# Branch B's first weights, its copies out of PSUM and the chunks' sum moved in the order of a hybrid decoder step

## The chip, the cores and the metric

The kernel runs on one core of one Trainium2 chip. The metric is the time of one execution on the device, in microseconds. Three runs of the kernel before took 989.81, 990.08 and 991.59 us; their median is 990.08 us.

## The reference

One layer of a decoder trunk is computed for 16 learned meta tokens with a prompt of 1024 positions, and for 8 sequences of 8 sample tokens; the model width is 1024.

```python
h = rmsnorm(x, norm_g)
z = jnp.einsum('btd,de->bte', h, w_in)
a_val, a_gate, a_silu, p_in, p_silu, g_a, g_b = jnp.split(z, idx, axis=-1)
u = a_val * jax.nn.sigmoid(a_gate)
c, new_conv = causal_depthwise_conv(u, buf_conv, conv_w, conv_b)       # width 31
c = jax.nn.silu(layernorm(c, ln_g, ln_b)) * jax.nn.silu(a_silu)
br_a = jnp.einsum('btc,cd->btd', c, w_conv_out)
pooled, new_pool = multiscale_pool(p_in, buf_pool, start_pos)          # windows 2, 4, 8, 16
q = jnp.einsum('btgc,gce->btge', pg, w_pool_mix).reshape(B_, T_, D_POOL)
q = q * pool_scale * jax.nn.silu(p_silu)
br_b = jnp.einsum('btc,cd->btd', q, w_pool_out)
merged = jax.nn.sigmoid(g_a) * br_a + jax.nn.sigmoid(g_b) * br_b
return x + jnp.einsum('btd,de->bte', merged, w_out), new_conv, new_pool
```

A final RMSNorm follows. The conv and pool states of the prompt and of the samples are outputs too. All inputs are fp32.

## The kernel before, in words

Channels lie on the 128 partitions, so a matrix of 1024 channels is eight chunks. The tokens are kept in two halves (`h` = 0, 1). Every fp32 product is made from three products of parts: each operand is split into a high part, rounded to the type that TensorE takes, and a low part, the rest; high times high, high times low and low times high are added in PSUM (`gemm`, L152). ScalarE's cast makes the high part. The low part comes in one of several ways: `split` (L119) has VectorE subtract at once; `split_late` (L124) has VectorE subtract some steps later; `split_dma` (L130) has ScalarE write the negated high part and a DMA of GpSimd's queue add the source onto it.

PSUM is four tiles of two banks (`bank2`). They are handed out in the order of the program: a new one takes the tile whose last reader came earliest in that order, and its first matmul waits for this reader.

The program is written out in one order by hand, and each engine executes its own instructions in that order. Three helpers make it. `step(us)` stands after each half product of TensorE: it counts a step, adds `us` to a planned TensorE clock and runs what is due. `defer(n, f)` makes `f` due n steps later; what is due in one step runs in the order in which it was deferred. `fill(until)` takes VectorE's background work (a queue `todo` of groups with planned costs: the taps of the depthwise conv, then the layer norm of branch A) until the planned VectorE clock is 1.5 us ahead of the planned TensorE clock; without an argument it takes everything that is queued.

The stages around the change:

- The pairs (L919 to L960). Most of the input projection is made in 22 pairs of column blocks with seven products each (`seven`); the last pair is `s3` (tiles `px_s`, `pv_s`, `py_s`). Beside them VectorE works at the conv. `load_q` reads branch B's `q` back from DRAM, `split_q` splits it. `po[d]` are the eight blocks of branch B's projection, `co[d]` those of branch A's (`Block.load` is two SP loads of 256 KB, `Block.split` makes the operands, tiles `raw_po` and `w_po`).
- Branch B's projection (L1052 to L1072). For each of eight blocks `d` and both halves: two half products of 24 matmuls into one PSUM tile (`ppo`), a `step` after each; then ScalarE copies the tile to SBUF (`zpo`), and SP stores it a step later (`d_tb`), to be read again at the merge. The `fill` calls in this loop place the rest of the conv, the sum over the chunks, the mean (`pt_mean`: an all-ones product), the centring and the squares, the variance (`pt_var`), and the first part of `finish_a`. The sum of the chunks that were stored lies in DRAM (`csum`); `load_sum` reads it, and queues `summing`, which adds the chunks that were kept, and after it the group that begins the mean.
- `finish_a` is `root` (the reciprocal root, and `scale` of chunk 0) and `branch_a(0)` to `branch_a(8)`. `branch_a(i)` scales chunk i+1 (VectorE multiplies, ScalarE takes the Silu), makes the low parts that are left over from the chunk before, loads the gate `lsa` two chunks ahead, multiplies chunk i by its gate and splits it into `cx[i]`.
- After the loop the tail takes what is left:

```python
while todo or due:
    fill()
    step(0.0)
```

- The merge (L1122 on): the first four products of branch A, blocks 0 and 1 with both halves, are made together, k by k, in all four PSUM tiles (`pco`); the other twelve follow one by one. VectorE multiplies each by its gate (L1147) and adds branch B's. Then come the output projection (`pwo`), the residual and the norm.

Of the kernel before, what the change touches and what calls it, by code (L numbers as in the profile page):

```python
# [32 lines left out]
H2 = HP + HS  # L33
# [36 lines left out]
def hybrid_trunk_kernel(  # L70
# [22 lines left out]
    act, dve, pe, pool, sp = nc.scalar, nc.vector, nc.tensor, nc.gpsimd, nc.sync  # L93
# [8 lines left out]
    def slot(name, shape=(T2,), dt=F32):  # L102
        return sl.tile([P, *shape], dt, tag="slot", name=name, bufs=NSLOT)


    def bank2(name):
        return ps2.tile([P, 2, 512], F32, tag="bank2", name=name, bufs=4)
# [34 lines left out]
    def half(name, n=HT, dt=F32):  # L142
        return wp.tile([P, n], dt, tag="z", name=name, bufs=NZ, padded_shape=[P, HT])
# [4 lines left out]
    def v3(ap, n):  # L148
        return ap.rearrange("p (a b) -> p a b", b=n)


    def gemm(out, w, xs, units, ks, first, last):  # L152
        for k in ks:
            for i, (a, b) in enumerate(((0, 0), (0, 1), (1, 0))):
                for u, (lo, hi) in enumerate(units):
                    pe.matmul(  # L156
                        out[:, u, : hi - lo],
                        w(k, a),
                        xs(k, b)[:, lo:hi],
                        start=first and k == ks[0] and i == 0,  # L160
                        stop=last and k == ks[-1] and i == 2,
                        skip_group_check=True,
                    )
# [5 lines left out]
    def defer(steps, run):  # L169
        due.append((clock["step"] + steps, run))  # L170

    def step(us):
        clock["step"] += 1
        clock["pe"] += us
        for x in [x for x in due if x[0] <= clock["step"]]:
            due.remove(x)
            x[1]()
# [147 lines left out]
    for i in range(NF, NX):  # L325
        ps = bank2(f"pp{i}0")
# [79 lines left out]
    def push(group, soon=False):  # L406
        todo.insert(1 if soon and todo else len(todo), deque(group))

    def fill(until=None):
        while todo and (until is None or clock["dve"] < until + LAG):  # L410
            if not todo[0]:
                todo.popleft()
                continue
            cost, run = todo[0].popleft()
            clock["dve"] += cost
            run()
# [53 lines left out]
    def seven(w, units, put):  # L470
# [46 lines left out]
    d_pool, d_q, d_sga, d_sgb, d_sa, d_c, d_tb = (  # L517
        dram.tile([NK, P, 2, H2], F32, name=f"d_{x}") for x in ("pool", "q", "sga", "sgb", "sa", "c", "tb")
    )
# [278 lines left out]
    def of_half(t):  # L798
        return v3(t, H2 // 2)

    def fetch_half(src, h, name):
        t = half(f"{name}{h}", H2)
        sp.dma_start(out=t, in_=src[:, h])
        return t

    def gemm_half(name, w, xs, h, nk):
        ps = bank2(f"{name}{h}")
        gemm(ps, w, lambda k, s: xs[k][h][:, s], UNITS3, tuple(range(nk)), True, True)
        return ps[:, :, : H2 // 2]

    def operand(name, src, how):
        o = slot(name, (2, H2), F32R)
        how(o[:, 0], o[:, 1], src)
        return o
# [45 lines left out]
    po = [Block(w_po[d], f"po{d}") for d in range(NK)]  # L860
# [48 lines left out]
    def load_q(j):  # L909
        qraw[j] = [fetch_half(d_q[j], h, f"lq{j}") for h in range(2)]  # L910

    def split_q(j):
        q.append([operand(f"q{j}{h}", z, split if j > 5 else split_late) for h, z in enumerate(qraw.pop(j))])
# [5 lines left out]
    for n in range(len(pairs)):  # L919
        nxt = pairs[n + 1][1] if n + 1 < len(pairs) else iter(())  # L920
        if n + 1 == len(pairs):
            for j, t in enumerate((1, 1, 2, 2, 3, 4, 5, 5)):
                if j > 1:
                    defer(t - 2, lambda j=j: load_q(j)) if t > 2 else load_q(j)
                defer(t, lambda j=j: split_q(j))
            po[0].load()
            defer(2, lambda: po[0].split(split))
            defer(3, po[1].load)
        next(after, None)
        next(cur)  # L930
        if mix:
            tail = mix.part(0, 0)
        next(cur)
        if mix:
            mix.gate(*tail)
            mix.gate(*mix.part(0, 1))
            mix.split(1)
        if 0 <= n - first_q < 4:
            coming = Mix(n - first_q)
            coming.load(0)  # L940
            coming.load_w()
        next(nxt, None)
        next(cur)
        if mix:
            tails = [mix.part(1, 0), mix.part(1, 1)]
            for tail in tails:
                mix.gate(*tail)
        if n + 2 == len(pairs):
            load_q(0)
            load_q(1)  # L950
        next(cur)
        if coming:
            coming.split(0)
            coming.split_w()
            coming.load(1)
        next(nxt, None)
        next(nxt, None)
        mix, coming = coming, None
        after, cur = cur, nxt
# [6 lines left out]
    def load_sa(i):  # L966
        if i < NK:
            lsa[i] = [fetch_half(d_sa[i], h, f"lsa{i}") for h in range(2)]


    def load_conv(lo, hi):
        for i in range(lo, hi):
            if getattr(chunks[i], "stored", False):
                conv[i] = slot(f"lc{i}", (2, H2))
                sp.dma_start(out=conv[i], in_=d_c[i])

    def load_sum():
        norm["sum"] = slot("lcsum", (2, H2))
        sp.dma_start(out=norm["sum"], in_=csum[0])
        todo.insert(max(len(todo) - 1, 0), deque(summing))  # L980
        push([(1.3, lambda: begin_totals("mean", squares_, norm.pop("parts"), [NK - 1]))])

    def sum_rest(i):
        if not chunks[i].stored:
            conv[i] = chunks[i].c
            dve.tensor_tensor(norm["sum"], norm["sum"], conv[i], ALU.add)
# [5 lines left out]
    def begin_totals(name, work, parts_, more):  # L992
        for i in more:
            if i not in conv:
                conv[i] = chunks[i].c
            parts_ = parts_ + total_parts(conv[i], H2, f"{name}{i}")

        def run():
            norm[name] = total_products(parts_, H2, name)
            push(work)  # L1000

        defer(1, run)
# [16 lines left out]
    def scale(i):  # L1019
        if i < NK:  # L1020
            dve.tensor_tensor(conv[i], conv[i], norm["rstd"], ALU.mult)
            act.activation(conv[i], conv[i], AF.Silu, bias=col(OFF_LB, i), scale=col(OFF_LG, i))
# [3 lines left out]
    def branch_a(i):  # L1026
        scale(i + 1)
        while low:
            low.popleft()()
        if i == NK:  # L1030
            return
        load_sa(i + 2)
        cx.append([])
        for h in range(2):
            src = conv[i][:, h]
            dve.tensor_tensor(src, src, lsa[i][h], ALU.mult)
            if i in (1, 3, 5):
                cx[i].append(operand(f"cx{i}{h}", src, split_dma))
            else:
                o = slot(f"cx{i}{h}", (2, H2), F32R)  # L1040
                act.copy(o[:, 0], src)  # L1041
                low.append(
                    lambda o=o, src=src: dve.tensor_tensor(o[:, 1], src, o[:, 0].bitcast(F32), ALU.subtract)
                )
                cx[i].append(o)
# [3 lines left out]
    squares_.append((1.3, lambda: begin_totals("var", finish_a, total_parts(norm[0], H2, "var"), [])))  # L1049
    summing = [(1.3, lambda i=i: sum_rest(i)) for i in range(NK - 1)] + [(1.3, sum_parts)]  # L1050

    for d in range(NK):  # L1052
        (po + co)[d + 2].load()
        (po + co)[d + 1].split(split_dma)
        for h in range(2):
            ps = bank2(f"ppo{d}{h}")
            for ks in (range(NQ), range(NQ, NK)):
                gemm(ps, po[d], lambda k, s: q[k][h][:, s], UNITS3, tuple(ks), ks[0] == 0, ks[0] > 0)
                step(T_PRODUCT)
                if ks[0] == 0 and d > 0:  # L1060
                    fill(clock["pe"])
            z = half(f"zpo{d}{h}", H2)
            act.copy(of_half(z), ps[:, :, : H2 // 2])  # L1063
            defer(1, lambda d=d, h=h, z=z: sp.dma_start(out=d_tb[d][:, h], in_=z))
            if d == 0:
                load_conv(h * 4, h * 4 + 4)
            if d == 1 and h == 0:
                load_sum()
            if d == 7 and h == 0:
                co[1].split(split_dma)  # L1070
                co[2].load()
            fill(clock["pe"])  # L1072
# [49 lines left out]
    for d in range(NK):  # L1122
# [16 lines left out]
        for h in range(2):  # L1139
            if d < 2:  # L1140
                ps = early[d, h][:, :, : H2 // 2]
            else:
                ps = gemm_half(f"pco{d}", co[d], cx, h, NK)
# [170 lines left out]
```

## Time and profile before

| what | value |
|---|---|
| median of three runs | 990.08 us |
| the profiled execution, its own time | 992.53 us |
| its span | 990.7 us |
| TensorE matmuls, busy | 947.3 us, 96% |
| VectorE busy | 771.8 us, 78% |
| ScalarE busy | 492.1 us, 50% |
| GpSimd busy | 185.7 us, 19% |
| mean granted TensorE clock | 0.976 of full speed |

The busy time of TensorE counts matmuls that overlap each other's start and drain, so it says when TensorE had work, not how fast it was. The granted clock is 1.00 at 2.4 GHz and 0.50 at 1.2 GHz. In the rows below a time is in us from the start of the span. In a timeline a row begins with the start and the duration of a run of like instructions; the bracket at its end is the time in which the engine stood idle before it, and what released it.

### The profile page before, as it was taken

What the parts mean: (1) busy time and instruction counts of PE and PEld (TensorE: products, weight loads), DVE (VectorE), ACT (ScalarE), POOL (GpSimd) and SP (SyncE); (2) the same over time, 40 slices, a digit from 0 to 9 for tenths busy, and PEclk for the clock granted to TensorE, in tenths of its full rate; (3) what the DMA queues carried; (4) which work ended last, traced back from release to release, by engine and by line L of the source; (5) the groups of instructions that cost most, each with busy time, mean ns of one, the idle gap of its engine ahead of it and who ended that gap; (6) DMA issues with size and microseconds to landing.
All of it is one profiled execution on the core that took longest, in us unless ns stands there. A gap on an engine that the chain in (4) does not pass through costs nothing.

```text
span 990.7 us, 18094 instructions
## 1 busy us (share of the span) xinstructions
PE 947.3 (96%) x7040; PEld 924.0 (93%) x7040; DVE 771.8 (78%) x1009; ACT 492.1 (50%) x834; POOL 185.7 (19%) x218
## 2 busy tenths in 40 slices
PE   9999997999999999999999999979999399999996
PEld 8999997999999999999999999969998399998885
DVE  6568959996988998999999999667985858664343
ACT  7655155556446555656556565544247842233111
POOL 0001322323232213223233322302202110000000
PEclk9999998999999999999999999979999599999998
DMA  8323797797968887888979899688547688652223
GB/s 315 131 81 100 235 267 136 169 223 185 230 134 220 208 208 185 227 232 212 235 173 239 179 243 209 183 294 241 142 114 199 192 220 280 189 187 93 85 75 106
DMA packets 104646, 187.61 MB, mean 189 GB/s; under 512 B 21872, under 2 KB 25328, under 8 KB 104560
## 3 DMA queue, kind: packets, MB, share of 16 engines
q1 hardware_dynamic: 70720, 121.98, 37.8%
q0 software_dynamic: 24624, 46.57, 27.4%
q10 hardware_dynamic: 9216, 17.90, 4.8%
q8 instruction: 55, 0.90, 0.4%
q14 instruction: 31, 0.25, 0.1%
HBM read 93.92 MB, written 48.71 MB: 144 GB/s over the span
## 4 chain that ended last, share of the span: by engine, by line
PE 68%; DVE 12%; DMA 9%; ACT 5%; issue 5%; SPq 1%; ACTq 0%; DVEq 0%; POOL 0%; POOLq 0%
PE pco L156 10%; PE pp L156 7%; PE px_b L156 5%; PE px_a L156 5%; PE pwo L1187 4%; PE px_s L156 4%; PE px_v L156 4%; PE px_g L156 4%; DVE c L690 4%; PE ppo L156 3%; PE px_q L156 2%; PE pv_b L156 2%; PE pv_a L156 2%; PE pv_v L156 2%; PE pmix L156 2%
## 5 line engine op out<-in xcount | busy, mean ns | idle before, releaser
L690 DVE SCALAR_TENSOR_TENSOR c<-ce,pv,c 128x1024 f32<-128x1024 f32 x240 | 308.2, 1284 | 11.4 <-ACT c L667 6.2
L156 PE MATMUL pco<-cx,w_co 128*128 128x272 f32 x768 | 102.4, 297 | 16.7 <-ACT cx L1041 12.0
L156 PEld LDWEIGHTS pco<-cx,w_co 128*128 128x128 f32 x768 | 101.3, 197 | 17.7 <-ACT cx L1041 12.2
L156 PE MATMUL ppo<-q,w_po 128*128 128x272 f32 x768 | 96.8, 288 | 0.6 <-DMA w_po<-raw_po 0.6
L156 PEld LDWEIGHTS ppo<-q,w_po 128*128 128x128 f32 x768 | 96.3, 188 | 0.8 <-DMA w_po<-raw_po 0.8
L1187 PE MATMUL pwo<-wo,mx 128*128 128x512 f32 x336 | 79.2, 393 | 0.0
L1187 PEld LDWEIGHTS pwo<-wo,mx 128*128 128x128 f32 x336 | 63.1, 188 | 14.7
L156 PE MATMUL pp<-xg,wh_p 128*128 128x276 f32 x384 | 65.4, 291 | 0.5 <-DVE xg L232 0.3
L156 PEld LDWEIGHTS pp<-xg,wh_p 128*128 128x128 f32 x384 | 54.8, 188 | 1.5 <-DVE xg L232 0.8
L120 ACT CAST mx<-ga 128x544 fp32r<-128x544 f32 x16 | 10.4, 647 | 63.9 <-DVE ga L1148 63.9
L1206 DVE TENSOR_TENSOR xr<-pwo,xr 128x1024 f32<-128x1024 f32 (+1 forms) x9 | 9.9, 1106 | 39.1 <-PE pwo L1187 19.9
L1169 ACT ACTIVATE sq<-xr 128x1024 f32<-128x1024 f32 (+1 forms) x9 | 8.7, 964 | 63.2 <-DVE xr L1206 63.2
L156 PE MATMUL pp<-xg,wl_p 128*128 128x276 f32 x192 | 40.0, 290 | 0.0
L156 PEld LDWEIGHTS pp<-xg,wl_p 128*128 128x128 f32 x192 | 30.2, 188 | 0.0
L1063 ACT COPY zpo<-ppo 128x544 f32<-128x544 f32 x16 | 9.8, 612 | 39.2 <-PE ppo L156 39.1
L133 POOL DMA_DIRECT2D w_po<-raw_po x14 | 12.1, 868 | 88.1 <-ACT w_po L132 85.9
L1147 DVE TENSOR_TENSOR ga<-pco,ga 128x544 f32<-128x544 f32 x16 | 11.5, 722 | 19.2 <-PE pco L156 19.2
L156 PE MATMUL px_g<-tT,woq_g 128*128 128x276 f32 x144 | 21.8, 314 | 4.8 <-ACT py_g L489 4.8
L156 PE MATMUL pmix<-px,m 128*128 128x272 f32 x192 | 26.0, 288 | 0.0
L156 PEld LDWEIGHTS px_g<-tT,woq_g 128*128 128x128 f32 x144 | 21.1, 212 | 5.0 <-ACT py_g L489 5.0
L156 PE MATMUL px_q<-tT,woq_q 128*128 128x272 f32 x192 | 25.5, 288 | 0.3 <-ACT py_q L489 0.3
L156 PE MATMUL px_b<-tT,woq_b 128*128 128x272 f32 x192 | 25.4, 288 | 0.0
(421 smaller groups left out, 2266.9 us busy)
## 6 DMA issues: line engine op xcount, KB each, us to landing
lraw<-d_raw SPq DMA_DIRECT2D x16, 276.0 KB, 3.4
d_pool<-pool SPq DMA_DIRECT2D x8, 544.0 KB, 4.6
lp<-d_pool SPq DMA_DIRECT2D x16, 272.0 KB, 4.7
lq<-d_q SPq DMA_DIRECT2D x16, 272.0 KB, 5.6
d_tb<-zpo SPq DMA_DIRECT2D x16, 272.0 KB, 2.3
lsa<-d_sa SPq DMA_DIRECT2D x16, 272.0 KB, 4.7
tb<-d_tb SPq DMA_DIRECT2D x16, 272.0 KB, 3.4
gb<-d_sgb SPq DMA_DIRECT2D x16, 272.0 KB, 3.7
```

What stands on the lines that cost most here:

```text
L120: act.copy(dst_h, src)
L133: pool.dma_start(out=dst_l, in_=src, accum_op=ALU.add)
L156: pe.matmul(out[:, u, : hi - lo], w(k, a), xs(k, b)[:, lo:hi], start=first and k == ks[0] and i == 0, stop=last and k == ks[-1] and i == 2 ...
L690: dve.scalar_tensor_tensor(c, s, wk, c, ALU.mult, ALU.add)
L1063: act.copy(of_half(z), ps[:, :, : H2 // 2])
L1147: dve.tensor_tensor(of_half(ga), ps, of_half(ga), ALU.mult)
L1169: act.activation(sq[:rows, c], xr[:, c], AF.Square, accum_out=a1 if ns[0] else a0)
L1187: pe.matmul(ps[:, n - ns[0]], x(k), wo[k][n][w], start=(k == 0 and s == 0), stop=(k == NK - 1 and s == len(passes) - 1),)
L1206: dve.tensor_tensor(v3(xr[:, c], 512), ps[:, : len(ns)], v3(xr[:, c], 512), ALU.add)
```

## The change

Five edits in one. `po[0].load` moves from the beginning of the last pair to the last part of the pair before, ahead of the first two `load_q`; `po[0].split` is due in step 3 of the last pair instead of step 2. `load_sum` only loads, and is called two steps of branch B's loop earlier, at (d, h) = (0, 1) instead of (1, 0); what it queued is queued by `begin_norm`, at (1, 1). Chunk 1's `cx` is split by ScalarE and VectorE instead of `split_dma`. The copy of each `ppo` out of PSUM is deferred by one step (`put_po`), and its store by one step more.

```diff
@@ -923,8 +923,7 @@
                 if j > 1:
                     defer(t - 2, lambda j=j: load_q(j)) if t > 2 else load_q(j)
                 defer(t, lambda j=j: split_q(j))
-            po[0].load()
-            defer(2, lambda: po[0].split(split))
+            defer(3, lambda: po[0].split(split))
             defer(3, po[1].load)
         next(after, None)
         next(cur)
@@ -946,6 +945,7 @@
             for tail in tails:
                 mix.gate(*tail)
         if n + 2 == len(pairs):
+            po[0].load()
             load_q(0)
             load_q(1)
         next(cur)
@@ -977,6 +977,8 @@
     def load_sum():
         norm["sum"] = slot("lcsum", (2, H2))
         sp.dma_start(out=norm["sum"], in_=csum[0])
+
+    def begin_norm():
         todo.insert(max(len(todo) - 1, 0), deque(summing))
         push([(1.3, lambda: begin_totals("mean", squares_, norm.pop("parts"), [NK - 1]))])
 
@@ -1034,7 +1036,7 @@
         for h in range(2):
             src = conv[i][:, h]
             dve.tensor_tensor(src, src, lsa[i][h], ALU.mult)
-            if i in (1, 3, 5):
+            if i in (3, 5):
                 cx[i].append(operand(f"cx{i}{h}", src, split_dma))
             else:
                 o = slot(f"cx{i}{h}", (2, H2), F32R)
@@ -1048,6 +1050,12 @@
     squares_ = [(2.7, lambda i=i: centre(i)) for i in range(NK + 1)]
     squares_.append((1.3, lambda: begin_totals("var", finish_a, total_parts(norm[0], H2, "var"), [])))
     summing = [(1.3, lambda i=i: sum_rest(i)) for i in range(NK - 1)] + [(1.3, sum_parts)]
+
+
+    def put_po(d, h, ps):
+        z = half(f"zpo{d}{h}", H2)
+        act.copy(of_half(z), ps[:, :, : H2 // 2])
+        defer(1, lambda: sp.dma_start(out=d_tb[d][:, h], in_=z))
 
     for d in range(NK):
         (po + co)[d + 2].load()
@@ -1059,13 +1067,13 @@
                 step(T_PRODUCT)
                 if ks[0] == 0 and d > 0:
                     fill(clock["pe"])
-            z = half(f"zpo{d}{h}", H2)
-            act.copy(of_half(z), ps[:, :, : H2 // 2])
-            defer(1, lambda d=d, h=h, z=z: sp.dma_start(out=d_tb[d][:, h], in_=z))
+            defer(1, lambda d=d, h=h, ps=ps: put_po(d, h, ps))
             if d == 0:
                 load_conv(h * 4, h * 4 + 4)
-            if d == 1 and h == 0:
+            if d == 0 and h == 1:
                 load_sum()
+            if d == 1 and h == 1:
+                begin_norm()
             if d == 7 and h == 0:
                 co[1].split(split_dma)
                 co[2].load()
```

## Rows read from the trace of the kernel before

**Rows 1.** TensorE's waits, 560 to 800 us: waiter, releaser, total us, times, longest.
```profile
PE pco L156 <- ACT cx L1041: 12.0, 1, 12.0
PE px_s L156 <- ACT c_s L479: 7.4, 1, 7.4
PE pco L156 <- DMA cx<-lc: 4.5, 2, 2.8
PE pt_mean L201 <- ACT sumh_mean L120: 0.7, 1, 0.7
PE pt_var L201 <- ACT sumh_var L120: 0.6, 1, 0.6
PE ppo L156 <- DMA w_po<-raw_po: 0.6, 1, 0.6
PE pt_mean L201 <- DVE suml_mean L121: 0.4, 1, 0.4
PE pt_var L201 <- DVE suml_var L121: 0.4, 1, 0.4
```

**Rows 2.** Timeline of TensorE, 776 to 813 us.
```profile
778.58 0.82 PE L156 MATMUL pco<-cx,w_co 128*128 128x272 f32 x2 [12.03 <-ACT cx L1041]
...
787.17 1.73 PE L156 MATMUL pco<-cx,w_co 128*128 128x272 f32 x6 [2.81 <-DMA cx<-lc]
790.55 22.66 PE L156 MATMUL pco<-cx,w_co 128*128 128x272 f32 x157 [1.64 <-DMA cx<-lc]
```

**Rows 3.** One window: length, busy us (instructions) by engine, TensorE clock, DMA share, GB/s.
```profile
812.00:885.00 73.00, 73.00 (x586) 73.00 (x585) 51.17 (x78) 20.14 (x35) 0.00 (x0) 1.00 0.66 207
```

**Rows 4.** Timeline of all engines, 776 to 812 us.
```profile
776.20 0.59 ACT L1063 COPY zpo<-ppo 128x544 f32<-128x544 f32 x1
...
777.08 7.17 SPq L803 DMA_DIRECT2D lsa<-d_sa  x6
...
778.81 1.36 DVE L1043 TENSOR_TENSOR cx<-lc,cx 128x544 fp32r<-128x544 f32 x2
...
784.35 0.84 SPq L1064 DMA_DIRECT2D d_tb<-zpo  x1
...
800.08 1.23 ACT L1041 CAST cx<-c 128x544 fp32r<-128x544 f32 x2 [1.57 <-DVE c L1036]
...
811.36 0.73 DVE L1147 TENSOR_TENSOR ga<-pco,ga 128x544 f32<-128x544 f32 x1 [8.60 <-PE pco L156]
```

**Rows 5.** Timeline of all engines, 612 to 676 us.
```profile
632.91 6.89 SPq L803 DMA_DIRECT2D lq<-d_q  x8
...
639.91 4.19 SPq L359 DMA_DIRECT2D raw_po<-in_w_po  x2
...
648.22 0.65 ACT L125 CAST q<-lq 128x544 fp32r<-128x544 f32 x1 [0.55 <-DMA lq<-d_q]
648.96 1.28 ACT L120 CAST w_po<-raw_po 128x512 fp32r<-128x512 f32 x2
649.61 1.35 DVE L121 TENSOR_TENSOR w_po<-raw_po,w_po 128x512 fp32r<-128x512 f32 x2 [11.75 <-ACT w_po L120]
...
654.06 0.61 ACT L479 COPY c_s<-px_s 128x544 f32<-128x544 f32 x1 [0.45 <-ACT zs L606]
...
654.73 5.67 PE L156 MATMUL px_s<-hx,woq_s 128*128 128x272 f32 x24 [7.39 <-ACT c_s L479]
...
657.16 0.72 DVE L502 SCALAR_TENSOR_TENSOR c_s<-pv_s,c_s 128x544 f32<-128x544 f32 x1
...
660.24 3.18 PE L156 MATMUL pv_s<-tT,wod_s 128*128 128x272 f32 x24
```

**Rows 6.** DMA issues: queue, operation, count, KB each, median us to landing.
```profile
lq<-d_q SPq DMA_DIRECT2D x16, 272.0 KB, 5.6
```

**Rows 7.** Timeline of all engines, 676 to 716 us.
```profile
679.02 0.40 SPq L979 DMA_DIRECT2D lcsum<-d_csum  x1
...
689.76 1.29 DVE L986 TENSOR_TENSOR lcsum<-lcsum,c 128x1088 f32<-128x1088 f32 x1 [5.84 <-DMA lcsum<-d_csum]
```

## The prediction, written before the changed kernel had run

> **What bounds the kernel now.** I read the page's busy shares first: TensorE is busy for nearly all of the span, so a change can only take away or add TensorE waits, or time at the lower of its two clocks (1.2 instead of 2.4 GHz). So the second view was the list of TensorE's own waits over the stretch that the change touches (560 to 800 us) [rows 1]. The reader is to see two large ones and several small ones: 12.0 us before branch A's product `pco`, 7.4 us in the last pair `s3`, 4.5 us on the two accumulating DMAs of `cx`, and pieces of 0.4 to 0.7 us at the two all-ones products and at one weight load. Third came TensorE's order of time around the 12 us gap [rows 2]. It ends at 778.58, the next waits are for `cx<-lc` DMAs, and from 790.55 there is none. Fourth, one window of the stage after that [rows 3]: TensorE is busy 73.00 of 73.00 us at full clock, 586 matmuls, or 0.125 us each. So whatever moves the end of the first four `pco` products moves the end of the kernel by as much. That end is found so: VectorE takes the first of the four at 811.36 [rows 4]; the other three have 18 matmuls left (6 each for the last k), 18 x 0.125 = 2.2 us, so 813.6 us.
>
> **The deferred copy out of PSUM.** This is the edit that decides. Fourteen of the copies are merely half a product later, and four PSUM tiles hide that. The last one, `ppo(7,1)`, is different. `put_po` is deferred by one step, but after the last product the next `step` stands in the tail loop, behind a `fill()` without limit, which first writes out all that is left of branch A. The trace shows this order already: the store of `zpo(7,1)`, deferred by one step, is issued at 784.35, after the last loads of `lsa` (the six from 777.08 on), which belong to the latest chunks [rows 4]. In the kernel before, the copy itself is ahead of that `fill`: ScalarE runs it at 776.20, between the first and the second Silu [rows 4]. After the change it is ScalarE's last instruction of the stage, behind the casts of chunk 7, which start at 800.08 and take 1.23 for two [rows 4]. `ppo(7,1)` holds one of the four tiles, and the first thing that branch A asks for is all four at once; the one freed last goes to `pco(1,1)`. TensorE takes its work in order, so after k = 0 of the three other products (18 matmuls) it waits for that copy.
>
> The price, step by step. Last cast done: 800.08 + 1.23 = 801.31. Chunk 1's low part moves to VectorE (below): + 1.36. The copy: one like that of 776.20, 0.6. That is 803.3, less S, by which branch A starts earlier. Then 192 - 18 = 174 matmuls at 0.125, 21.75 us, and a start at the lower clock: after the wait of 7.39 us, 24 matmuls took 5.67 us [rows 5], where 24 at 0.125 take 3.0; I add 2.5. End: 827.5 - S, against 813.6: **13.9 - S** slower.
>
> The rule that speaks for the edit: the Trainium skill (Perfetto Trace Analysis, Matmuls) says that independent groups of matmuls should rotate through PSUM banks, so that emptying one overlaps the matmuls of the next. By it a copy half a product late costs nothing, and this edit's term would be 0 in place of 13.9. The trace agrees for products in steady rotation (the list of [rows 1] has no TensorE wait for a `zpo` copy); no run here shows yet the case in which all four tiles are asked for together.
>
> **S: what branch A gains before that.** (a) `po[0].load` goes ahead of `load_q(0)` on SP's queue, from 639.91 to about 632.9 [rows 5], and its two issues push the `lq` loads back by some 0.8 us. VectorE waits 11.75 us for the ScalarE cast of this weight, until 649.61 [rows 5]. But the split is a step later too, so its casts now stand on ScalarE behind the copy `c_s` of 654.06 and the casts of `q4`, and its VectorE part still stands ahead of the low parts of `q2` and `q3`. ScalarE's casts of `q2`, `q3` wait for their DMAs until 648.22 + 0.65 [rows 5]; then follow `zs`, `c_s` (about 650.7), two casts of `q4`, two of `w_po` (0.64 each; the first ends at 652.5). So VectorE's stall is split in two (for `q0`, and from about 645 to 652.5), not removed. TensorE's fourth product of `s3` starts at about 650.7 instead of 654.73, but its last, 660.24 before, needs VectorE's `c_s` operation (657.16 to 657.9), which stands behind two `w_po` parts, four of `q` and one tap: about 658.5. At best 1.7 us earlier, and the half clock after two short idles takes that back. Bounds: all of the stall and its slow restart go, + 7.39 + 2.5 = 9.9; or the two weight loads delay the `lq` loads by their full size: eight loads of 272 KB [rows 6] landed from 632.91 to 648.22, so two of 256 KB are 3.6 us, - 3.6. I take 0, the row of `c_s` on VectorE being nearest.
>
> Under the rule of ring order, the Trainium skill (DMA: Bandwidth & Descriptors, Queues, rings and completion order) has each DMA engine take descriptors in the order of its ring, so the weight's packets would all go first; the sum would then be by the lower bound. The trace has 8 to 9 us from issue to use for the later `lq` loads, which fits a backlog but does not prove the order.
>
> (b) The sum of the chunks: issued at 679.02, VectorE waited 5.84 us for it until 689.76 [rows 7]. It is now issued some 4 us earlier on SP and first needed half a product later or more; that stall goes. VectorE is then ahead of TensorE at the all-ones product of the mean, where TensorE waits 0.7 + 0.4 [rows 1]. That is all that reaches TensorE, for its place in TensorE's order stays: **1.1**. Bounds 0 and 1.1: if VectorE kept the stall, the 1.1 stays. (c) ScalarE's casts for the variance stand behind the copy of `ppo(7,0)` and `co[1]`'s split; now ahead of that copy. TensorE waits there 0.6 + 0.4 [rows 1]: **0.9**, bounds 0 and 1.0. What stays is the chain from the variance to the first `cx` (TensorE's 12.0 us), because `pt_var` keeps its place in TensorE's order. The wait of 0.6 for `w_po` [rows 1] I leave; it can go or double. S = 0 + 1.1 + 0.9 = **2.0**.
>
> (d) Chunk 1's low part leaves ScalarE's second pass and POOL's DMA for two VectorE operations like those of 778.81, 1.36 for two [rows 4]. VectorE is nearly without a gap there, so all later chunks are 1.36 later (in the sum above). What it buys, the wait of 2.81 at 787.17 and part of 1.64 at 790.55 [rows 2], lies under the new wait for the copy and is worth nothing.
>
> **Sum.** 13.9 - 2.0 = 11.9 us slower. The profiled execution took 992.53 us (span 990.7 and 1.8 around it), 2.4 above the median of 990.08, and a difference inside it carries over: 990.1 + 11.9 = **1002.0 us**.
>
> **The rivals.** *One: the copy is not late* (faster). Place: the fourth tile at k = 0 of branch A. If the copy is written out before the remaining chunks, or another tile is free, TensorE goes on as before; the point is whether the copy ends before TensorE has done its 18 matmuls, some 4 us after it restarts. Then the gain is S = 2.0 plus the first `cx` wait 2.8, less 1.4 for the chunks behind it: 990.1 - 3.4 = 986.7. For it: rows of the steady rotation. Against it: the store at 784.35. Chance 8%. *Two: the stall in `s3` goes altogether* and the copy is late as forecast: S = 9.9 + 2.0, 13.9 - 11.9 = 2.0 slower, 992.1. For it: the load really is 7 us earlier. Against it: the split's new place behind `c_s`. Chance 7%, nearly half of it within 0.2%. *Three: the weight loads delay `lq`* and the last pair ends 3.6 later: S = -1.6, 15.5 slower, 1005.6. For it: the 9 us that those loads already take. Chance 7%. The forecast: 78%.
>
> **How the numbers follow.** The range runs from half of rival two's extra S (S = 7.4: 6.5 slower, 996.6) to rival three with a restart 1 us slower (1006.5): 996.5 to 1006.5; it leaves out rival one, rival two and little else. 0.2% (2 us) is about what a measurement can tell from no change. Faster 0.08 (rival one), same 0.03 (part of two), slower 0.89.
>
> **What would show it.** Right: in the new profile TensorE starts `pco` near 776.5, stops after about 18 matmuls, and the list of its waits names ScalarE's `zpo` copy with some 20 us; that copy stands on ScalarE after the last cast of `cx`, near 801; VectorE's first merge is near 823 instead of 811.36; `lcsum` is no longer waited for; the wait in `s3` is split, not gone. Wrong: the last `zpo` copy stands before the second Silu, or TensorE has no wait for it; or `ppo` starts at 655 rather than near 663; or VectorE, free of both stalls, brings the mean forward in a way that moves `pt_mean` in TensorE's order, which I hold to be fixed by the plan.

## The result

The changed kernel takes 1002.06 us (median of four runs, 1000.38 to 1002.35), the kernel before 990.69 beside it (also four runs): a ratio of 1.011 with a 95% interval of 1.0095 to 1.0125, so 9.4 to 12.4 us slower. The forecast was 1002.0, 11.9 slower. The profiled execution took 1000.38 us (span 998.6).

TensorE's waits from 560 to 815 us of the changed kernel; they answer to [rows 1]:

```profile
PE pco L156 <- ACT zpo L1057: 19.7, 1, 19.7
PE pco L156 <- ACT cx L1043: 11.5, 1, 11.5
PE px_s L156 <- ACT c_s L479: 4.5, 1, 4.5
PE pv_s L156 <- DVE c_s L502: 2.0, 1, 2.0
PE pco L156 <- DVE cx L1045: 0.7, 1, 0.7
```

One new wait stands on top: 19.7 us for ScalarE's `zpo` copy. The waits at the two all-ones products, for `w_po` and for the `cx` DMAs are gone; the 7.4 us of `px_s` are now 4.5 there and 2.0 at `pv_s`. TensorE's order around the gap, against [rows 2]:

```profile
771.97 0.82 PE L156 MATMUL pco<-cx,w_co 128*128 128x272 f32 x2 [11.54 <-ACT cx L1043]
773.47 3.68 PE L156 MATMUL pco<-cx,w_co 128*128 128x272 f32 x16 [0.68 <-DVE cx L1045]
796.83 33.34 PE L156 MATMUL pco<-cx,w_co 128*128 128x272 f32 x251 [19.69 <-ACT zpo L1057]
```

18 matmuls (2 + 16), then the stop, then none. What it waited for, in the timeline of all engines, against [rows 4]:

```profile
795.04 1.23 ACT L1043 CAST cx<-c 128x544 fp32r<-128x544 f32 x2 [1.57 <-DVE c L1038]
...
796.17 0.60 ACT L1057 COPY zpo<-ppo 128x544 f32<-128x544 f32 x1
...
796.81 0.32 SPq L1058 DMA_DIRECT2D d_tb<-zpo  x1
...
818.32 0.73 DVE L1155 TENSOR_TENSOR ga<-pco,ga 128x544 f32<-128x544 f32 x1 [16.72 <-PE pco L156]
```

The copy of `ppo(7,1)`, at 776.20 before, is now ScalarE's first instruction after the casts of chunk 7, and TensorE starts 0.06 us after its end (796.17 + 0.60 = 796.77, 796.83). The first merge is at 818.32 instead of 811.36.

Executions differ by some microseconds ahead of any edit: the product that ran at 632.15 in the kernel before (the `pv_s` product with `wod` of the last pair but one) runs between 629.5 and 633.2 in the profiles of this study, at 629.49 in this one. So stages are compared from that mark on. In us, by TensorE's starts and VectorE's first merge:

| kernel | mark to `ppo` | `ppo` to `pt_mean` | `pt_mean` to `pt_var` | `pt_var` to first merge |
|---|---|---|---|---|
| before | 31.1 | 66.9 | 31.4 | 49.9 |
| changed | 31.7 | 66.1 | 29.0 | 62.1 |
| copies in place | 30.1 | 66.1 | 29.8 | 49.9 |
| deferral alone | 31.2 | 66.1 | 32.6 | 62.0 |
| last copy in place | 31.7 | 66.0 | 29.0 | 48.2 |
| three tiles early | 31.5 | 66.1 | 29.0 | 48.3 |
| first weights alone | 30.1 | 66.1 | 31.4 | 49.1 |
| sum alone | 30.5 | 66.7 | 29.8 | 48.9 |
| weights split first | 28.1 | 66.1 | 29.0 | 48.8 |
| the same kernel once more | 27.3 | 66.1 | 29.0 | 50.1 |
| chunk 1 by DMA, last copy in place | 31.4 | 66.1 | 29.0 | 48.5 |
| the parts together, chunk 1 by DMA | 28.2 | 66.1 | 29.0 | 48.8 |

How small a difference can be read, the table shows itself. One kernel was profiled twice (weights split first): its first column differs by 0.8 and its last by 1.3, the two in the middle by less than 0.1. And six of the kernels (changed, copies in place, last copy in place, three tiles early, first weights alone, chunk 1 by DMA) run the same program up to `ppo`, and their first column goes from 30.1 to 31.7.

The changed kernel is 9.6 us later at the first merge, counted from the mark (+ 0.6 - 0.8 - 2.4 + 12.2), and 0.9 in what follows it, which no edit touches.

### The profile page after: what moved, and what is told of

It reads as the page before. It is cut to its first block, busy times and chain, and to the rows that moved or that the text cites. A ratio compares the mean times of both kernels' runs of the same rounds, so it can differ in the third digit from the quotient of the medians.

```text
span 998.6 us, 18072 instructions
## 1 busy us (share of the span) xinstructions
PE 944.1 (95%) x7040; PEld 922.6 (92%) x7040; DVE 773.1 (77%) x1011; ACT 491.0 (49%) x832; POOL 185.7 (19%) x216
## 4 chain that ended last, share of the span: by engine, by line
PE 76%; DVE 10%; DMA 6%; ACT 4%; issue 3%; SPq 1%; ACTq 0%; DVEq 0%
PE pco L156 10%; PE ppo L156 9%; PE pp L156 7%; PE px_b L156 5%; PE px_a L156 5%; PE pwo L1195 4%; PE px_q L156 4%; PE px_v L156 4%; PE px_g L156 4%; PE px_s L156 3%; PE pv_b L156 2%; PE pv_a L156 2%; PE pmix L156 2%; PE pv_s L156 2%; PE pv_v L156 2%
## 5 line engine op out<-in xcount | busy, mean ns | idle before, releaser
L156 PE MATMUL pco<-cx,w_co 128*128 128x272 f32 x768 | 100.4, 294 | 31.9 <-ACT zpo L1057 19.7
L133 POOL DMA_DIRECT2D w_po<-raw_po x14 | 12.2, 870 | 83.4 <-PE ppo L156 47.6
L156 PE MATMUL px_s<-tT,woq_s 128*128 128x272 f32 x192 | 25.4, 288 | 0.0
L156 PE MATMUL px_a<-tT,woq_a 128*128 128x272 f32 x192 | 25.4, 288 | 0.0
```

Source lines behind the costliest of these rows:

```text
L133: pool.dma_start(out=dst_l, in_=src, accum_op=ALU.add)
L156: pe.matmul(out[:, u, : hi - lo], w(k, a), xs(k, b)[:, lo:hi], start=first and k == ks[0] and i == 0, stop=last and k == ks[-1] and i == 2 ...
```

## The experiments

The theory is that of the prediction: the late last copy makes the loss. Rival one: chunk 1's low part on VectorE makes the loss, by delaying every later chunk. Rival two: the weight loads ahead of `lq` make it.

**The copies back in place, the rest of the change kept.**

```diff
-            defer(1, lambda d=d, h=h, ps=ps: put_po(d, h, ps))
+            put_po(d, h, ps)
```

> The changed kernel with every copy of ppo out of PSUM back where it was; the other four edits stay. Theory (the loss is the last copy, which holds the fourth PSUM tile until ScalarE has done all of branch A): TensorE has no wait for a zpo copy, the 19.7 us wait goes, and the rest of the change shows what it is worth: about 987 us, 985 to 989. Rival one (the loss comes from chunk 1's low part on VectorE, which delays every later chunk of branch A): still 999 or more. Rival two (the loss comes from the weight loads ahead of lq in the last pair): still 999 or more, with ppo starting later than in the kernel before.

Measured: 989.53 us, ratio 0.9984 [0.9973, 0.9996]. The loss is gone with the deferral, so both rivals fall; the time lies half a microsecond above the expected span. TensorE's waits for `pco` and at the variance:

```profile
PE pco L156 <- ACT cx L1043: 12.0, 1, 12.0
PE pco L156 <- DMA cx<-lc: 5.8, 2, 5.5
...
PE pt_var L201 <- ACT sumh_var L120: 0.6, 1, 0.6
PE pt_var L201 <- DVE suml_var L121: 0.4, 1, 0.4
```

The wait for `cx` DMAs that chunk 1 had (4.5 us in [rows 1]) has not gone: it is now 5.8, for chunk 3.

**The deferral alone, in the kernel before.**

```diff
+    def put_po(d, h, ps):
...
-            z = half(f"zpo{d}{h}", H2)
-            act.copy(of_half(z), ps[:, :, : H2 // 2])
-            defer(1, lambda d=d, h=h, z=z: sp.dma_start(out=d_tb[d][:, h], in_=z))
+            defer(1, lambda d=d, h=h, ps=ps: put_po(d, h, ps))
```

> The kernel before with the deferred copies alone. Theory: one TensorE wait of about 20 us for the last zpo copy, 12 to 13 us slower by it, less 1.5 to 2 that the deferral gives back at the variance: about 1001.5 us, 1000 to 1003. Rivals one and two: within 2 us of the kernel before.

Measured: 1003.84 us, ratio 1.0121 [1.0103, 1.0138]; 0.8 us above the expected span. Three of TensorE's waits:

```profile
PE pco L156 <- ACT zpo L1055: 18.3, 1, 18.3
PE pco L156 <- ACT cx L1041: 11.5, 1, 11.5
...
PE pt_mean L201 <- ACT sumh_mean L120: 1.1, 1, 1.1
```

One edit makes the whole loss and a little more; the other four give back some 2 us. Part of this is at the mean: without the moved sum, TensorE waits there 1.1 us for ScalarE's casts instead of the 0.7 of [rows 1], and the stage from `pt_mean` to `pt_var` is 1.2 longer than before (32.6 for 31.4).

**One copy of sixteen back in place.**

```diff
-            defer(1, lambda d=d, h=h, ps=ps: put_po(d, h, ps))
+            if (d, h) == (NK - 1, 1):
+                put_po(d, h, ps)
+            else:
+                defer(1, lambda d=d, h=h, ps=ps: put_po(d, h, ps))
```

> The changed kernel with one copy of sixteen put back: that of ppo(7,1), made right after its product; the other fifteen stay deferred. Theory: the wait of 19.7 us goes and what the deferral gives at the two all-ones products stays: about 986 us, 984 to 988, some 1 us under the kernel with all copies in place. If it were the deferral as such, and not the last copy: fifteen sixteenths of the loss stay, 1000 us or more.

Measured: 987.86 us, ratio 0.9968 [0.9956, 0.998]. All of TensorE's waits from 560 to 820:

```profile
PE pco L156 <- ACT cx L1043: 12.0, 1, 12.0
PE pco L156 <- DMA cx<-lc: 5.3, 2, 4.9
PE px_s L156 <- ACT c_s L479: 4.5, 1, 4.5
PE pv_s L156 <- DVE c_s L502: 2.5, 1, 2.5
PE pco L156 <- DVE cx L1045: 0.2, 1, 0.2
```

So it is the last copy alone. Beside the moved sum the other fifteen deferred copies cost nothing, and they take TensorE's wait at the variance away: the median is 1.7 us lower than with all copies in place, and the stage from `pt_mean` to `pt_var` 0.8 shorter (29.0 for 29.8).

**Three tiles together instead of four, the copy as late as in the changed kernel.**

```diff
-            early = {(d, h): bank2(f"pco{d}{h}") for d in range(2) for h in range(2)}
+            early = {(d_, h): bank2(f"pco{d_}{h}") for d_, h in ((0, 0), (0, 1), (1, 0))}
...
-            if d < 2:
+            if (d, h) in early:
```

> The changed kernel, all copies deferred, but branch A's first product group takes three PSUM tiles together, and pco(1,1) is made afterwards by itself. The last copy stays as late on ScalarE, near 796. Theory (it is the fourth tile that TensorE waits for): the wait of 19.7 us goes although the copy is just as late; TensorE follows the chunks of cx to about 801 and then makes 48 matmuls (6 us) for the fourth: end of the group near 808 to 811 instead of 820.6, in all 987 to 991 us. If TensorE waited for ScalarE for another reason than the tile (its casts or Silus), the time stays near 1002.

Measured: 989.23 us, ratio 0.9972 [0.9959, 0.9986]. The copies of this kernel (count, shortest/median/longest in ns, first and last start), and TensorE's waits for `pco`:

```profile
L1057 ACT COPY zpo<-ppo x16: 589/610/616, 670.8 to 797.6; 128x544 f32<-128x544 f32 x16
```

```profile
PE pco L156 <- ACT cx L1043: 11.5, 1, 11.5
PE pco L156 <- DMA cx<-lc: 4.6, 2, 4.0
...
PE pco L156 <- DVE cx L1045: 1.8, 2, 1.2
```

The last copy starts at 797.6, as late as in the changed kernel (166.5 us after the mark for 166.7), and TensorE does not wait for it. The four products end near 809, in the expected span: an estimate from 170 matmuls done by the first merge at 805.93 and 22 more at 0.125. That separates the two halves of the cause: the copy is late because of its place in ScalarE's order, and the lateness costs because the fourth tile is asked for at k = 0.

**The first weights alone, in the kernel before.**

```diff
-            po[0].load()
-            defer(2, lambda: po[0].split(split))
+            defer(3, lambda: po[0].split(split))
...
+            po[0].load()
             load_q(0)
```

> The kernel before with the first edit alone: po[0] loaded in the last pair but one, its split a step later. Theory (VectorE's stall of 11.75 us is cut in two, not removed, and branch B's first product starts as early as before): ppo starts within 1 us of 31 us after the start of the last pair's product that runs at 632.15 in the kernel before; the time is within 1.5 us of the kernel before. Rival (the stall goes, as the edit's place suggests): VectorE's waits between 630 and 660 sum to under 5 us instead of 12, ppo starts 5 us or more earlier, 984 to 986 us. Other rival (the weight loads delay lq): ppo starts 2 to 4 us later, 992 to 994 us.

Measured: 990.55 us, ratio 0.9997 [0.9985, 1.001]; `ppo` starts 30.1 us after the mark instead of 31.1, which is within what the first column of the table shows for one and the same program. VectorE's two largest waits around the last pair:

```profile
DVE w_po L121 <- ACT w_po L120: 6.5, 1, 6.5
DVE q L127 <- ACT q L125: 6.3, 3, 4.7
```

6.5 and 6.3 in place of the 11.75 of [rows 5]: cut in two. Both rivals fall.

**Chunk 1 by the accumulating DMA again, last copy in place.**

```diff
-            if i in (3, 5):
+            if i in (1, 3, 5):
```

> The changed kernel with the last copy in place, and chunk 1's cx again split by ScalarE and an accumulating DMA. Prediction: under the wait for the copy this edit was worth nothing and cost 1.4; with the wait gone it shows what it buys. Theory: TensorE again waits for chunk 1's DMA (2.8 us) and starts again at the lower clock, but chunk 3's DMA is then issued 1.4 earlier: the kernel is slower than the one with the last copy in place by 0 to 3 us, 988 to 991 us. Rival (VectorE's extra 1.36 us are the larger part): 1 to 2 us faster than it, 986 us.

Measured: 986.99 us, ratio 0.9961 [0.9945, 0.9977], 0.9 under the kernel with the last copy in place (measured on another chip), against the theory. It did not repeat (below).

**The weights split first in the last pair, last copy in place.**

```diff
         if n + 1 == len(pairs):
+            defer(1, lambda: po[0].split(split))
             for j, t in enumerate((1, 1, 2, 2, 3, 4, 5, 5)):
...
-            defer(3, lambda: po[0].split(split))
```

> The changed kernel with the last copy in place, and po[0]'s split due in the last pair's first step, ahead of the splits of q, where its loads have landed already. Theory (the stall of VectorE stayed because the casts stand on ScalarE behind the copy c_s): VectorE's wait of 6.6 us for the w_po casts falls under 2 us, TensorE's wait of 2 to 2.5 us before the last product of s3 goes, its wait of 4.5 us before the fourth stays (that is for q2 and q3's loads): ppo starts 2 to 4 us earlier than in the kernel with the last copy in place, and the time falls by as much, to 984 to 986 us. Rival (VectorE waits for lq whatever the order of the weight): same time as that kernel, 988 us.

Measured: 984.60 us, ratio 0.9943 [0.9923, 0.9963]. TensorE's waits, and two rows of the last pair (ScalarE's casts of the weight, VectorE's `c_s` operation):

```profile
PE pco L156 <- ACT cx L1043: 12.0, 1, 12.0
PE pco L156 <- DMA cx<-lc: 5.5, 2, 5.1
PE px_s L156 <- ACT c_s L479: 4.5, 1, 4.5
PE pco L156 <- DVE cx L1045: 0.2, 1, 0.2
```

```profile
639.54 1.14 ACT L120 CAST w_po<-raw_po 128x512 fp32r<-128x512 f32 x2
...
649.71 0.72 DVE L502 SCALAR_TENSOR_TENSOR c_s<-pv_s,c_s 128x544 f32<-128x544 f32 x1
```

`ppo` starts 28.1 us after the mark, 3.6 earlier than with the split in step 3. VectorE still waits 4.7 us for these casts, which was expected to fall under 2; but the wait now lies where VectorE would have waited for `q0` (4.7 us in the changed kernel), the casts no longer stand behind the copy `c_s` of the fourth product, and TensorE's wait at `pv_s` is gone.

**The sum alone, in the kernel before.**

```diff
-            if d == 1 and h == 0:
+            if d == 0 and h == 1:
                 load_sum()
+            if d == 1 and h == 1:
+                begin_norm()
```

> The kernel before with the third edit alone: the chunks' sum loaded two steps earlier, and what uses it queued later. Prediction: VectorE's wait of 5.84 us for lcsum goes, of which 1.1 us reach TensorE (its waits at the mean's all-ones product): 989.6 us, 988.5 to 990.7. Rival (all of VectorE's gain reaches the end): 985 us. TensorE's waits before pt_mean should be gone from the list, and pt_mean should keep its place among the ppo matmuls.

Measured: 988.48 us, ratio 0.9976 [0.9965, 0.9987], 2.4 us faster by it (1.3 to 3.5), more than the 1.1 expected. TensorE's waits:

```profile
PE pco L156 <- ACT cx L1043: 12.0, 1, 12.0
PE px_s L156 <- ACT c_s L479: 7.2, 1, 7.2
PE pco L156 <- DMA cx<-lc: 4.2, 2, 2.2
PE pt_var L201 <- ACT sumh_var L120: 0.6, 1, 0.6
PE pt_var L201 <- DVE suml_var L121: 0.4, 1, 0.4
PE ppo L156 <- DMA w_po<-raw_po: 0.4, 1, 0.4
```

No wait at `pt_mean` is left, and its place is kept. The stage from `pt_mean` to `pt_var` is 1.6 shorter (31.4 to 29.8); that is what reaches TensorE of VectorE's 5.84. The rest of the 2.4 is inside the interval and stays open.

**The parts that gain, together**, once with chunk 1 by DMA and once with its low part on VectorE (the second is the kernel with the weights split first, run again beside the first).

> The parts that gained, together: the changed kernel with the last copy in place, po[0]'s split first in the last pair, and chunk 1's cx by an accumulating DMA as in the kernel before. Theory (the three stand in different stages and add up): the time of the kernel with the weights split first less the 0.9 us that chunk 1 by DMA gave: 983.7 us, 982 to 985.5; TensorE's waits for cx DMAs sum to about 4.2 us instead of 5.5. Rival (branch A's chunks bound the end of the group whichever way they are split, so what comes earlier is waited away): 984.6 us or more.

> The same with chunk 1's low part on VectorE, on the same chip for comparison: 984.6 us as before, 983 to 986; the wait for chunk 3's DMA is about 5 us. Theory: 0.5 to 1.5 us slower than with chunk 1 by DMA. Rival: no difference.

Measured: 985.10 us, ratio 0.9939 [0.9922, 0.9955], and 984.36 us, ratio 0.9927 [0.9912, 0.9941]. TensorE's waits for `cx` DMAs sum to 5.0 us in the first, where 4.2 was expected; the one for chunk 3's in the second is 5.9, where some 5 was. The first time lies in the span of the theory and in that of its rival. Here, on one chip, chunk 1 by DMA is 0.7 slower, before it was 0.9 faster: chunk 1's edit makes no difference that these runs can tell. The version with the last copy in place and the weights split first beats both kernels, the one before by some 6 to 7 us.

## Why the prediction was right, step by step

**The deferred copy.** Right in place, cause and size. The stage from `pt_var` to the first merge grew by 12.2 us, although the variance's products inside it became 0.9 shorter (1.87 to 1.00) and the chain from them to the first `pco` 0.5 shorter (15.20 to 14.72; the copy no longer stands on ScalarE ahead of chunk 0's casts, which the prediction did not count): 13.6 for the copy against 13.9. From TensorE's restart to the end of the group are 818.32 - 796.83 + 2.2 = 23.7 us, against 24.25. The signs came 4.5 to 5 us earlier than written (the copy at 796.17 for 801, the first merge at 818.32 for 823): 2.7 of it lies ahead of the mark, the rest is the larger S (below). Of the sixteen copies fifteen, and not fourteen, are merely half a product late. The rule of rotating tiles of the Trainium skill (Perfetto Trace Analysis, Matmuls), by which the term would have been 0, holds for fifteen of the sixteen copies: the kernel with only the last one in place has no wait for a `zpo` copy. For the sixteenth it fails, because two things come together: the copy stands behind the rest of ScalarE's stage, and the next group asks for all four tiles at once. With either taken away (last copy in place, three tiles early) the wait is gone.

**The first weights.** Right: 0 was taken. Measured were + 0.6 in the changed kernel and - 1.0 alone, but kernels that are the same up to `ppo` spread from 30.1 to 31.7 with this edit and from 30.5 to 31.2 without it, so the runs show no difference. The timeline of the last pair in the changed kernel:

```profile
630.33 0.83 SPq L359 DMA_DIRECT2D raw_po<-in_w_po  x2
...
631.22 23.13 SPq L803 DMA_DIRECT2D lq<-d_q  x16
...
645.47 2.10 ACT L125 CAST q<-lq 128x544 fp32r<-128x544 f32 x3 [0.54 <-DMA lq<-d_q]
...
648.54 0.61 ACT L479 COPY c_s<-px_s 128x544 f32<-128x544 f32 x1 [0.45 <-ACT zs L606]
...
649.21 5.30 PE L156 MATMUL px_s<-hx,woq_s 128*128 128x272 f32 x24 [4.53 <-ACT c_s L479]
650.15 1.14 ACT L120 CAST w_po<-raw_po 128x512 fp32r<-128x512 f32 x2
650.80 1.30 DVE L121 TENSOR_TENSOR w_po<-raw_po,w_po 128x512 fp32r<-128x512 f32 x2 [6.62 <-ACT w_po L120]
...
655.75 0.72 DVE L502 SCALAR_TENSOR_TENSOR c_s<-pv_s,c_s 128x544 f32<-128x544 f32 x1
...
656.52 4.81 PE L156 MATMUL pv_s<-tT,wod_s 128*128 128x272 f32 x24 [2.01 <-DVE c_s L502]
```

The loads go out at 630.33, some 7 us earlier from the mark; the casts wait behind `c_s` until 650.15, VectorE for them until 650.80, and TensorE's `pv_s` for VectorE's `c_s` of 655.75. `pv_s` starts 1.1 us earlier from the mark (27.0 for 28.1), and then its 24 matmuls take 4.81 us where they took 3.18 [rows 5]: the granted clock is 0.62 to 0.67 there. So the lower clock takes the gain back, as forecast. With the copies in place the same product ran at a granted clock of 1.00, in 3.28 us; that is the 30.1 of the table.

The `lq` loads did come later: the casts of `q2` and `q3` end 18.1 us after the mark (645.47 + 2.10), 16.7 before [rows 5]; in all nine profiles with this edit it is 17.9 to 18.1, in the three without 15.9 to 16.7. Of the 1.4 us between these two kernels, 1.0 is that the loads are issued later (631.22 is 1.7 after the mark, 632.91 was 0.8), which leaves 0.4 of the 3.6 that the lower bound allowed. By the ring order that the Trainium skill states (DMA: Bandwidth & Descriptors, Queues, rings and completion order) the sum would have gone by that bound; it did not, and the runs neither prove nor refute the order itself. TensorE's fourth product still starts 2.9 us earlier from the mark (19.7 for 22.6), and rival three falls.

**The sum.** Direction right, size off: 1.1 taken, 1.6 measured, since the waits listed for the two matmuls are less than the time that the group of 16 lost (3.61 us before, 2.01 after). And one thing was missed. VectorE's stall did not simply go:

```profile
672.19 0.44 SPq L979 DMA_DIRECT2D lcsum<-d_csum  x1
...
685.93 1.28 DVE L988 TENSOR_TENSOR lcsum<-lcsum,c 128x1088 f32<-128x1088 f32 x1
...
691.39 0.61 ACT L1057 COPY zpo<-ppo 128x544 f32<-128x544 f32 x1 [4.53 <-PE ppo L156]
691.90 1.20 ACT L120 CAST sumh_sum<-lcsum 128x544 fp32r<-128x544 f32 x2
...
692.59 1.36 DVE L121 TENSOR_TENSOR suml_sum<-lcsum,sumh_sum 128x544 fp32r<-128x544 f32 x2 [5.37 <-ACT sumh_sum L120]
```

It adds the sum at 685.93 without a wait, and then waits 5.37 us for ScalarE's casts, which stand behind the deferred copy of 691.39, and that behind TensorE. VectorE was early enough for the mean all the same. This wait was 0.8 in the kernel before; with the sum moved but no copy deferred it is 3.6 (the sum alone) and 3.9 (the copies in place).

**The variance.** 0.9 taken, 1.4 measured (2.45 us from the start of TensorE's wait to the end of the eight matmuls before, 1.00 after), for the same reason as at the mean. With 0.8 at `ppo`'s second weight, which was left out, and the 0.5 of the chain, and less the 0.6 of the first weights, S is about 4 instead of 2.0 (13.6 - 9.6).

**Chunk 1.** Right that it is worth nothing under the copy. Its 1.36 us in the sum was 1.1 in the profiles: from the first `pco` to the end of the late copy are 24.8 us in the changed kernel and 23.7 with the deferral alone. (After it TensorE ran at a granted clock of 0.50 for some 5 us with the deferral alone and for some 3 in the changed kernel, which hid this at the first merge.) Rival one's price was wrong: it counted 1.4 us for this edit once the copy is not late. The kernel with the last copy in place, which is rival one's case, took 987.9 and not 986.7 although S was larger, because the wait for chunk 1's DMA comes back at chunk 3's (4.5 us in all before, 5.3 there).

**The sum and the range.** The mechanism was right; that forecast and measurement agree within 0.1 us is luck. By the stages the copy's 13.6 less the S of 4 makes 9.6, and 0.9 more comes after the first merge, where the same code took 179.3 to 180.9 us in the profiles of this study: 10.5 rather than 11.9. The medians differ by 11.4; the 0.9 between is inside the interval and stays open. The forecast also started from 990.08, where four runs give 990.69. And the lower end of the range has a slip: half of rival two's extra 9.9 makes an S of 6.95, not 7.4, and so 997.0 instead of 996.5. The measured time is far from either.

## What to carry to other kernels

Before you defer the release of a buffer by "one step", look for the last one of the loop: behind the loop a step may stand after a flush of everything else that is queued. A group that takes all buffers at once needs the last release, whatever slack the rotation had before. And when a load is moved ahead of use, follow its consumer too: a load 7 us earlier was worth nothing that the runs can tell until its split was moved ahead of the work that blocked the engine that splits.

## What the runs showed that was not expected

A stall that is taken from an in-order engine can come back where it next meets an engine that is behind: VectorE waited 5.84 us for the sum and 0.8 for ScalarE's casts before, and 5.37 us for these casts after. And work that no edit touches took up to 3.7 us more or less from one execution to the next: the same TensorE product, some 630 us into the program, started between 629.49 and 633.18.
